# s4's quarter sums on ScalarE's queue, x11 t4 as the fourth quarter product, and first products by pairs of row tiles

## The chip, the cores and the metric

The kernel runs on one core of a Trainium2 chip. The metric is the device time of one launch in microseconds. Three runs before the change took 1567.93, 1563.51 and 1567.34 us, a median of 1567.34 us.

## What is computed

```python
def reference(a, b, alpha):        # a, b: 4096 x 4096 float32, alpha = 0.01
    x = np.matmul(a, b)
    return np.where(x > 0, x, alpha * x)
```

## The kernel before

**Seven products for eight.** Outside its first block the kernel works through 15 regions of the output, each 1024 x 1024 and named (g, j) by its block row and block column, in the order of the list `regions`: (0, 1) (0, 2) (0, 3), then (1, 2) (1, 0) (1, 1) (1, 3), (2, 2) (2, 0) (2, 3) (2, 1), (3, 2) (3, 0) (3, 1) (3, 3). A region is a 2 x 2 block product, A in blocks a11, a12, a21, a22 of 512 rows by 2048 of K, B in blocks B11 to B22 of 2048 by 512. It is done by Winograd's form of Strassen's scheme: sums s1 to s4 of A's blocks, sums of B's blocks made in place on VectorE (`b_sum`, L561), and seven block products instead of eight, numbered 0 to 6 in the code and called first to seventh here where the code does so (`sixth_in_quarters`, `seventh_in_quarters`). All operands are float16, made from the float32 inputs on the way in.

One block product is 64 matmuls (L722) of a 128 x 128 tile of A against 512 columns of B: two tiles `k` of K (`ks`), eight chunks `c` in each, four row tiles `mt`. Each row tile has a PSUM bank of its own. Two sets of four banks alternate: `y` of a region are at `ybank`, `z` at `zbank`, and the next region's `ybank` is this one's `zbank`. Within a block product the order is chunk by chunk, and the four row tiles inside a chunk, so its first four matmuls want four different banks.

**Quarter products.** In the regions of groups g = 1 to 3 that are neither the last of their group nor the last of all, the seventh product (s4 times B22) is done by the same scheme once more, on quarters of 256 rows by 1024 of K and 1024 by 256: seven quarter products of 16 matmuls of 256 columns (`quarter_product`, L673) from quarters x, sums `sx(1)` to `sx(4)` of them, quarters b and sums `t(1)` to `t(4)` of them. In six of these nine regions, (1, 0) (1, 1) (2, 0) (2, 3) (3, 0) (3, 1), the sixth product (a22 times B21) is done in quarters too; the code calls that `both`. The text calls the last region of groups 1 and 2, (1, 3) and (2, 1), turning: there A's next block row is fetched by GpSimd's queue (L130) and transposed on VectorE (L139) between the other steps.

The quarter sums of a22 and s4 are made once a group, in the region that opens it, and kept in DRAM (`kept_qa`, `kept_qs`, stored by L658). The `both` regions load them again (`load_sums`, L667): a22's before product 3, s4's inside `sixth_in_quarters`, by `following(n)`, each of 512 KB into the room of a sum that the sixth has finished with. So a load of s4's sum waits for TensorE: sum 4 for the sixth's second quarter product, sum 2 for the fourth, sum 1 (in the room of `sq[4]`) for the fifth, sum 3 for the sixth.

**The seventh in quarters, before**, is seven quarter products in this order: x01 b10 onto y (banks 0 and 1, left columns); x00 b00 into `one`; sx4 b11 onto y (banks 0 and 1, right columns); sx2 t2 into `one`; sx1 t1 into `other`; sx3 b01 into `one`; x11 t4 onto y (banks 2 and 3, left columns). Between them ScalarE copies `one` out (L798, L801, L806) and VectorE adds `other` (L803, L807), then adds all four banks of y into the result (L810). `one` is bank 3 of `z` in the `both` regions and bank 0 in the three that open a group, `other` is bank 2. These are banks that the next region's first product writes. After it the code fetches B22 for the next region (`fetch_b`, on GpSimd's queue, L505, or SyncE's, L502, for the column whose float16 form is kept) and loads the sum s2 again (`load_s2`, L692).

**Queues.** The order of every engine is the order of the code, written out by hand; nothing is scheduled. Loads from `kept_q`, output stores (L820 in `leave`), and `load_s2` all stand in SyncE's queue (SP), in the code's order, and each waits there for its own data and room. GpSimd's queue (POOL) has the loads from the inputs that change type. ScalarE (ACT) issues two loads at the very start and none after that.

The adds that free `z` after product 1, `add(u1, z)`, and the others of that form are L815; product 3 writes these banks again.

Of the kernel before, what the change touches and what calls it, by code (L numbers as in the profile page):

```python
# [24 lines left out]
KC = 8  # L25
# [21 lines left out]
def kernel(  # L47
# [16 lines left out]
    nc = tc.nc  # L64
# [23 lines left out]
    x = small_pool.tile([P, 8], FP32, name="x")  # L88
# [114 lines left out]
    def new_bank(i):  # L203
        return psum_pool.tile([P, NT], FP32, name="ps", tag=f"ps{i}")
# [126 lines left out]
    order = [("b", 0), ("a", 0, 0, 1), ("a", 1, 0, 1), ("a", 2, 0, 1), ("a", 3, 0, 1)]  # L331
# [3 lines left out]
    for what, i, *more in order:  # L335
        if what == "a":
            r, tiles = more
            k = slice(r * rw, (r + 1) * rw)
# [7 lines left out]
    both = []  # L346
# [98 lines left out]
    for i in range(1, len(steps)):  # L445
        t, h, u, first, last = steps[i]
# [16 lines left out]
        t, h, u, first, last = steps[i]  # L463
# [90 lines left out]
    def operand(g, name, k):  # L554
        if name[0] == "s":
            return s[g, name, k]
        return at[g, int(name[1]) - 1, 2 * (int(name[2]) - 1) + k]
# [61 lines left out]
    kept_q = {name: dram_pool.tile([4, P, QUARTER], DT, name=f"kept_q{name}") for name in ("a22", "s4")}  # L619
# [42 lines left out]
        make(3, (0, 0), (1, 0), SUB)  # L662
        make(4, (0, 1), 2, SUB)

    def load_sums(name, to, which):
        for n in which:
            nc.sync.dma_start(to[n], kept_q[name][n - 1])  # L667

    def quarter_product(xq, yq, to, first=False):
        for c in range(KC):  # L670
            for m in range(2):
                rows = slice(m * P, (m + 1) * P)
                nc.tensor.matmul(  # L673
                    to[m], xq[:, c // 2, rows, c % 2], yq[:, c, :],
                    start=first and (c, m) == (0, 0), stop=c == KC - 1, skip_group_check=True,
                )

    def into(bank):
        return [bank[:, m * HALF:(m + 1) * HALF] for m in range(2)]
# [24 lines left out]
    for i, (g, j) in enumerate(regions):  # L704

        ks = (1, 0) if in_quarters else (0, 1)
        late_s2 = in_quarters
# [4 lines left out]
        zbank = 4 - ybank  # L712

        def product(n, banks, first):
            name, half, nt = PRODUCTS[n]
            todo = [(k, c) for k in ks for c in range(KC)]
            order = [(mt, k, c) for k, c in todo for mt in range(MT)]
            if final and n == 6:
                order = [(mt, k, c) for mt in range(MT) for k, c in todo]
            for mt, k, c in order:  # L720
                t = operand(g, name, k)
                nc.tensor.matmul(  # L722
                    banks[mt], a_cols(t, c, mt, t is first_a), B(half, nt, k)[:, c, :],
                    start=first and (k, c) == todo[0], stop=(k, c) == todo[-1], skip_group_check=not first,
                )
# [12 lines left out]
        def sixth_in_quarters(pairs, banks, v, y, tq, sq):  # L738


            b = quarters_of_b(i, 1, 0)
            x = quarters_of_a(g, "a22")
            one, other, third, fourth = banks
            t = lambda n: b_quarter(tq[n])
            sx = lambda n: a_quarter(sq[n])
            next_t, next_s = {}, {}
            y7 = quarters_of_b(i, 1, 1)

            def more(r, n, t):
                block = pairs[r][:, :, n * HALF:(n + 1) * HALF]  # L750
                nc.vector.tensor_add(block, pair(t), block)

            def following(n, room=None):
                next_s[n] = new_a16() if room is None else room
                load_sums("s4", next_s, (n,))

            quarter_product(x[0, 0], b[0, 0], into(one), True)
            add(v[:2], y[:2])
            more(0, 0, one)
            add(v[2:], y[2:])  # L760
            quarter_product(sx(1), t(1), into(other), True)
            more(1, 1, other)
            following(4)
            next_t[2] = tq[1]
            quarter_product(x[0, 1], b[1, 0], into(fourth), True)
            leave(v, 1, 1)
            quarter_product(sx(2), t(2), into(one))
            following(2)
            more(0, 1, one)
            sums_of_b(y7, next_t, (2,))  # L770
            more(0, 0, fourth)
            quarter_product(sx(4), b[1, 1], into(other))
            following(1, sq[4])
            next_t[4] = tq[2]
            sums_of_b(y7, next_t, (4,))
            more(0, 1, other)
            quarter_product(sx(3), b[0, 1], into(one))
            following(3)
            more(1, 0, one)
            more(1, 1, one)  # L780
            quarter_product(x[1, 1], t(4), into(third), True)
            more(1, 0, third)
            next_t[1] = tq[4]
            sums_of_b(y7, next_t, (1,))
            return next_t, next_s

        def seventh_in_quarters(y, one, other, tq, sq):

            pairs, kept = new_c(side)
            b = quarters_of_b(i, 1, 1)  # L790
            x = quarters_of_a(g, "s4")
            t = lambda n: b_quarter(tq[n])
            sx = lambda n: a_quarter(sq[n])
            block = lambda r, n: pairs[r][:, :, n * HALF:(n + 1) * HALF]
            onto = lambda r, n: [y[2 * r + m][:, n * HALF:(n + 1) * HALF] for m in range(2)]
            quarter_product(x[0, 1], b[1, 0], onto(0, 0))
            quarter_product(x[0, 0], b[0, 0], into(one), True)
            nc.scalar.copy(block(0, 0), pair(one))  # L798
            quarter_product(sx(4), b[1, 1], onto(0, 1))
            quarter_product(sx(2), t(2), into(one))  # L800
            nc.scalar.copy(block(0, 1), pair(one))  # L801
            quarter_product(sx(1), t(1), into(other), True)
            nc.vector.tensor_add(block(0, 1), pair(other), block(0, 1))  # L803
            quarter_product(sx(3), b[0, 1], into(one))
            for n in (1, 0):
                nc.scalar.copy(block(1, n), pair(one))  # L806
            nc.vector.tensor_add(block(1, 1), pair(other), block(1, 1))  # L807
            quarter_product(x[1, 1], t(4), onto(1, 0))
            for mt in range(MT):
                nc.vector.tensor_add(kept[mt], y[mt], kept[mt])  # L810
            return kept

        def add(acc, banks):
            for to, bank in zip(acc, banks):
                nc.vector.tensor_add(to, bank, to)  # L815
# [25 lines left out]
        y = [new_bank(ybank + mt) for mt in range(MT)]  # L841
        z = [new_bank(zbank + mt) for mt in range(MT)]
# [5 lines left out]
        both = in_quarters and not first_of_group  # L848
# [34 lines left out]
        u2_pairs, u2 = keep(y, 1 - side)  # L883
# [8 lines left out]
        if in_quarters:  # L892
            t = x_pool.tile([P, 4, QUARTER], DT, name="q", tag="x")
            tq, sq = {2: t[:, 0], 1: t[:, 1], 4: t[:, 2]}, {4: t[:, 3]}
# [7 lines left out]
        z = [new_bank(zbank + mt) for mt in range(MT)]  # L902
# [20 lines left out]
        if turning:  # L923
            new_s(g + 1, "s1")
            t = new_s(g + 1, "s2").rearrange("p k c m e -> p (k c m e)").bitcast(BF16)
            a21 = measure(i + 1, 0, 1, 0, t.rearrange("p (n w) -> p n w", n=4))
            a21.begin()
        if both:
            tq, sq = sixth_in_quarters(u2_pairs, [new_bank(zbank + mt) for mt in range(MT)], v, y, tq, sq)
# [12 lines left out]

        if not both:
            product(5, z, False)
            add(u2, z)
        fetch_b(i + 1, [(1, 0)], (1, 0) if both else ks)
        fetch_a(1, 1, slice(3))
        leave(u2, 1, 0)
# [8 lines left out]

        if in_quarters:

            kept_c = seventh_in_quarters(y, new_bank(zbank + (3 if both else 0)), new_bank(zbank + 2), tq, sq)  # L960
            fetch_b(i + 1, [(1, 1)], (1, 0))
            new_s(g, "s2")
            load_s2(g, 1)
            leave(kept_c, 0, 1)
        else:
            product(6, y, False)
            fetch_b(i + 1, [(1, 1)], ks)
            if final:
                even = nc.values_load(good[0:1, 0:1], min_val=0, max_val=1)
            _, kept_c = new_c(side)  # L970

            def store(mt):
                nc.sync.dma_start(place(g, 0, mt, j, 1), kept_c[mt])

            for mt in range(MT):
                nc.scalar.copy(kept_c[mt], y[mt])  # L976
                leaky(kept_c[mt])
                if not (final and mt == MT - 1):
                    store(mt)
# [5 lines left out]
    with inputs.Else():  # L985
        for m in range(M // RM):
            a_blocks = []
            for u in range(KU):
                t = a_pool.tile([P, KC // 2, RM, 2], BF16, name="a", tag=f"a{u // 2 + 1}{m % 2 + 1}")
                for mt in range(0, MT, 2):  # L990
                    to = lambda t0, t1: [t[:, :, (mt + t0) * P:(mt + t1) * P, :]]
# [4 lines left out]
            for n in range(N // NT):  # L996
                banks = [new_bank(n % 2 * 4 + mt) for mt in range(MT)]
                cols = slice(n * NT, (n + 1) * NT)
                for u in range(KU):
                    t = b_pool.tile([P, KC, NT], BF16, name="b", tag=f"b{u // 2 + 1}{n % 2 + 1}")  # L1000
# [8 lines left out]
                for mt in range(MT):  # L1009
                    t = c_pool.tile([P, 2, NT], FP32, name="c", tag=f"c{side}")[:, 0]  # L1010
# [38 lines left out]
```

## Time and the profile before

| | |
|---|---|
| median of three runs | 1567.34 us (1563.51 to 1567.93) |
| the profiled execution | 1564.15 us, span 1562.3 us |
| granted TensorE clock, mean | 0.999 |
| TensorE matmuls, busy | 1547.7 us, 7995 matmuls |
| VectorE busy | 1126.4 us |
| ScalarE busy | 373.5 us |
| 512-column matmuls, L722, from A and from sums | 752.6 + 503.2 us, 3456 + 2304 matmuls |
| loads of s4's quarter sums | 24 of 512 KB, median 10.4 us from issue to landing |
| loads of a22's quarter sums | 24 of 512 KB, median 6.3 us |

Times in the profile count from the span's start. A line of the timeline has start, length, engine, source line, operation and tiles, and in brackets the idle time before it with what ended it; a matmul's length is that of its whole pass through the array, so neighbours overlap, and the pace is read from the starts. In the windows view a line has, for each stretch, the busy time of each engine, then the granted clock, the DMA share and GB/s.

### The profile page before, as it was taken

How to read it: one execution, taken by the hardware profiler on the slowest of the kernel's cores; microseconds unless marked ns; L12 is line 12 of the kernel's file. 1: busy time of each engine (PE TensorE's matmuls, PEld its weight loads, DVE VectorE, ACT ScalarE, POOL GpSimd, SP SyncE). 2: the span in 40 equal slices, each digit the busy share in tenths (PEclk: the TensorE clock that was granted, in tenths of full speed). 3: DMA queues.
4: the chain of work that ended last, by engine and by line, in shares of the span. 5: the costliest groups of instructions: out<-in, count | busy, mean ns of one | idle time of the engine just before them, and what ended most of it. 6: DMA issues, size and time to landing. Idle time of an engine off the chain costs nothing. (4 is left out here: it accounts for less than half of the span.)

```text
span 1562.3 us, 20105 instructions
## 1 busy us (share of the span) xinstructions
PE 1547.7 (99%) x7995; PEld 779.9 (50%) x7995; DVE 1126.4 (72%) x1265; ACT 373.5 (24%) x390; POOL 299.7 (19%) x482
## 2 busy tenths in 40 slices
PE   9999999999999999999999999999999999999998
PEld 4444444444445456474444546547444454745543
DVE  4368758777984676965799587685879959678474
ACT  2201243612100314301111241420022143151230
POOL 5641110244002011023401102012340110202100
PEclk9999999999999999999999999999999999999999
DMA  9999694999829789499985959969996794978902
GB/s 243 187 212 193 140 285 149 186 202 189 294 63 272 171 180 273 125 256 213 185 291 144 273 126 231 228 150 275 208 220 225 176 266 105 272 179 187 272 27 84
DMA packets 206056, 310.75 MB, mean 199 GB/s; under 512 B 18049, under 2 KB 155521, under 8 KB 199042
## 3 DMA queue, kind: packets, MB, share of 16 engines
q0 software_dynamic: 149376, 141.59, 56.9%
q1 hardware_dynamic: 56290, 167.41, 28.9%
q8 instruction: 64, 1.05, 0.3%
q10 hardware_dynamic: 288, 0.39, 0.1%
q14 instruction: 38, 0.31, 0.1%
HBM read 354.42 MB, written 94.37 MB: 287 GB/s over the span
## 5 line engine op out<-in xcount | busy, mean ns | idle before, releaser
L722 PE MATMUL ps<-b,a 128*128 128x512 f16 x3456 | 752.6, 379 | 0.2 <-DVE c L815 0.2
L722 PEld LDWEIGHTS <-a 128*128 128x128 f16 x3456 | 338.2, 98 | 406.4 <-issue 0.8
L722 PE MATMUL ps<-b,s 128*128 128x512 f16 x2304 | 503.2, 379 | 0.0
L722 PEld LDWEIGHTS <-s 128*128 128x128 f16 x2304 | 225.4, 98 | 271.9
L561 DVE TENSOR_TENSOR b<-b 128x4096 f16<-128x4096 f16 x112 | 252.8, 2291 | 111.3 <-DMA b<-in_b_dram 104.5
L505 POOL DMA_DIRECT2D b<-in_b_dram x184 | 136.4, 746 | 931.4 <-PE ps L722 625.4
L735 ACT COPY c<-ps 128x512 f32<-128x512 f32 x180 | 92.3, 598 | 459.5 <-PE ps L722 398.3
L139 DVE STREAM_TRANSPOSE a<-a 128x512 uint32<-128x512 uint32 (+2 forms) x120 | 126.9, 1104 | 85.0 <-DMA a<-in_a_dram 83.9
L130 POOL DMA_DIRECT2D a<-in_a_dram x252 | 137.4, 552 | 201.4 <-DVE a L139 119.3
L815 DVE TENSOR_TENSOR c<-ps,c 128x512 f32<-128x512 f32 x156 | 97.1, 683 | 87.2 <-PE ps L722 58.1
L307 DVE SCALAR_TENSOR_TENSOR c<-c 128x512 f32<-128x512 f32 x240 | 149.6, 688 | 12.7 <-ACT c L976 10.0
L227 ACT ACTIVATE sq<-b 128x2048 bf16<-128x2048 f16 x64 | 119.2, 1909 | 113.5 <-DVE sq L236 89.3
L279 PE MATMUL ps<-b,a 128*128 128x512 f16 x512 | 113.0, 379 | 2.4 <-DVE part L318 1.3
L227 ACT ACTIVATE sq<-a 128x2048 bf16<-128x2048 f16 x48 | 89.0, 1910 | 109.2 <-DVE sq L236 87.5
L673 PEld LDWEIGHTS <-q 128*128 128x128 f16 x960 | 92.7, 98 | 16.5 <-DMA q<-kept_qs 5.8
L279 PEld LDWEIGHTS <-a 128*128 128x128 f16 x512 | 49.7, 98 | 63.5 <-issue 3.8
L798 ACT COPY c<-ps 128x512 f32<-128x512 f32 x9 | 5.3, 587 | 257.9 <-PE ps L673 257.9
L673 PE MATMUL ps<-b,q 128*128 128x256 f16 x480 | 56.4, 273 | 0.6 <-DMA q<-kept_qs 0.4
L673 PE MATMUL ps<-q,q 128*128 128x256 f16 x384 | 45.4, 273 | 0.8 <-DMA q<-kept_qs 0.8
L239 DVE TENSOR_TENSOR sq<-sq 128x2048 bf16<-128x2048 bf16 x27 | 33.1, 1226 | 17.1 <-ACT sq L227 17.1
L673 PEld LDWEIGHTS <-s 128*128 128x128 f16 x432 | 42.3, 98 | 5.5
L803 DVE TENSOR_TENSOR c<-ps,c 128x512 f32<-128x512 f32 x9 | 6.2, 692 | 43.7 <-issue 43.7
(94 smaller groups left out, 715.2 us busy)
## 6 DMA issues: line engine op xcount, KB each, us to landing
b<-in_b_dram POOLq DMA_DIRECT2D x192, 512.0 KB, 14.6
out_dram<-c SPq DMA_DIRECT2D x240, 256.0 KB, 6.0
a<-in_a_dram POOLq DMA_DIRECT2D x244, 128.0 KB, 5.3
b<-kept SPq DMA_DIRECT2D x24, 1024.0 KB, 7.9
s<-kept_s SPq DMA_DIRECT2D x18, 1024.0 KB, 7.3
q<-kept_qa SPq DMA_DIRECT2D x24, 512.0 KB, 6.3
q<-kept_qs SPq DMA_DIRECT2D x24, 512.0 KB, 10.4
b<-in_b_dram POOLq DMA_DIRECT2D x24, 256.0 KB, 9.4
```

Source lines behind the costliest of these rows:

```text
L130: nc.gpsimd.dma_start(a16[32 * q:32 * q + 32], src.rearrange("(g i) w -> i g w", i=32))
L139: nc.vector.transpose(part.rearrange("p c m e -> p c (m e)").bitcast(U32) .rearrange("p c (g i) -> p g c i", i=32), src[:, :, i * n:(i + 1 ...
L227: nc.scalar.activation(to, self.parts[n], SQUARE)
L239: nc.vector.tensor_add(total, total, self.held[3])
L279: nc.tensor.matmul(ps, a_cols(at[0, h, u], c, mt, (h, u) == (0, 0)), bt[0, u, nt][:, c, :], start=first, stop=last,)
L307: nc.vector.scalar_tensor_tensor(t, t, alpha, t, op0=MULT, op1=MAX if alpha <= 1 else MIN)
L505: nc.gpsimd.dma_start(t[:, c:c + 4, :], b_rows(j, u, c, 4, nt, g > 0))
L561: nc.vector.tensor_tensor(f(to), f(x0), f(x1), op)
L673: nc.tensor.matmul(to[m], xq[:, c // 2, rows, c % 2], yq[:, c, :], start=first and (c, m) == (0, 0), stop=c == KC - 1, skip_group_check=True,)
L722: nc.tensor.matmul(banks[mt], a_cols(t, c, mt, t is first_a), B(half, nt, k)[:, c, :], start=first and (k, c) == todo[0], stop=(k, c) == t ...
L735: nc.scalar.copy(kept[mt], banks[mt])
L815: nc.vector.tensor_add(to, bank, to)
```

## The change

Five edits go together.

1. `load_sums` takes a queue, and the loads of s4's quarter sums inside the sixth are issued by ScalarE.
2. In a region that follows one with quarter products, the first product (n == 0) goes, for each `k`, over all chunks for row tiles 0 and 1, then over all chunks for row tiles 2 and 3. The matmuls are the same.
3. In the seventh, x11 t4 moves from seventh to fourth place, so sx2 t2, sx1 t1 and sx3 b01 come one place later and sx3 b01 is last.
4. After a sixth that is not in quarters the adds of `z` go from bank 3 down to bank 0.
5. `one` is bank 3 of `z` in all nine regions.

```diff
-    def load_sums(name, to, which):
+    def load_sums(name, to, which, queue=nc.sync):
         for n in which:
-            nc.sync.dma_start(to[n], kept_q[name][n - 1])
+            queue.dma_start(to[n], kept_q[name][n - 1])
...
             order = [(mt, k, c) for k, c in todo for mt in range(MT)]
+            if n == 0 and late_s2:
+                order = [(mt, k, c) for k in ks for mts in ((0, 1), (2, 3)) for c in range(KC) for mt in mts]
...
-                load_sums("s4", next_s, (n,))
+                load_sums("s4", next_s, (n,), nc.scalar)
...
             quarter_product(sx(4), b[1, 1], onto(0, 1))
+            quarter_product(x[1, 1], t(4), onto(1, 0))
             quarter_product(sx(2), t(2), into(one))
...
             nc.vector.tensor_add(block(1, 1), pair(other), block(1, 1))
-            quarter_product(x[1, 1], t(4), onto(1, 0))
             for mt in range(MT):
...
             product(5, z, False)
-            add(u2, z)
+            add(u2[::-1], z[::-1])
...
-            kept_c = seventh_in_quarters(y, new_bank(zbank + (3 if both else 0)), new_bank(zbank + 2), tq, sq)
+            kept_c = seventh_in_quarters(y, new_bank(zbank + 3), new_bank(zbank + 2), tq, sq)
```

`late_s2` is true in a region whose predecessor ended in quarter products.

## The prediction

> **What bounds the kernel now.** I read the page first: TensorE is busy nearly all the time, so only its idle time can be won. The chain that ended last is two pieces at the very end and says nothing. The waits of TensorE come next; of its rows this one belongs to quarter products that load s4's sums.
>
> ```profile
> PE 1547.7 (99%) x7995; PEld 779.9 (50%) x7995; DVE 1126.4 (72%) x1265; ACT 373.5 (24%) x390; POOL 299.7 (19%) x482
> ...
> PE ps L673 <- DMA q<-kept_qs: 1.7, 5, 0.5
> ...
> DMA to landing us min/median/max: 7.4/10.6/12.8
> ```
>
> The wait is counted as the gap between modelled matmul ends and so is too small; the third line (the view of the tile kept_qs) says how long these loads take. The timeline of TensorE shows the true size, by start times. This is the seventh product of region (1, 1), from its second product on:
>
> ```profile
> 684.74 3.66 PE L673 MATMUL ps<-b,s 128*128 128x256 f16 x32
> 688.23 1.91 PE L673 MATMUL ps<-b,q 128*128 128x256 f16 x16
> 690.64 1.92 PE L673 MATMUL ps<-q,q 128*128 128x256 f16 x16 [0.50 <-DMA q<-kept_qs]
> 692.93 1.92 PE L673 MATMUL ps<-q 128*128 128x256 f16 x16 [0.38 <-DMA q<-kept_qs]
> 694.72 1.92 PE L673 MATMUL ps<-b,q 128*128 128x256 f16 x16
> 696.48 1.91 PE L673 MATMUL ps<-q,s 128*128 128x256 f16 x16
> 698.22 27.79 PE L722 MATMUL ps<-b,a 128*128 128x512 f16 x128
> ```
>
> A quarter product takes (688.23 - 684.74) / 2 = 1.745 us when nothing is late. Five lie between 688.23 and 698.22: 9.99 us instead of 8.73, so 1.26 us are lost, before sums 2, 1 and 3. The same stretch in the six regions with both products in quarters: 593.67 to 603.44, 688.23 to 698.22, 975.38 to 984.63, 1069.42 to 1078.75, 1355.33 to 1364.66, 1449.44 to 1458.55. Less 8.73 each, these lose 1.04, 1.26, 0.52, 0.60, 0.60 and 0.38, **4.40 us** in all. The three regions that open a group lose nothing here. Who issues these loads, and when:
>
> ```profile
> 676.20 0.32 SPq L667 DMA_DIRECT2D q<-kept_qs  x1
> 677.57 2.14 SPq L820 DMA_DIRECT2D out_dram<-c  x4
> 679.80 3.71 SPq L667 DMA_DIRECT2D q<-kept_qs  x3
> 687.41 2.14 SPq L820 DMA_DIRECT2D out_dram<-c  x4
> ```
>
> Sum 2 leaves at 679.80, 0.3 us after the fourth quarter product of the sixth (677.75 to 679.50) has given its tile free, and is behind four output stores in one queue; it releases TensorE at 690.64, 10.8 us later. In region (2, 3) the stores also hold up the issue itself, by about 1 us.
>
> **x11 t4 goes ahead of the three late users.** No matmul is added: 16 of them change place. Sums 2, 1 and 3 are released after the sixth's products 4, 5 and 6 and needed at places 4, 5 and 6 of the seventh; these become 5, 6 and 7, so each has 7 x 1.745 = 12.2 us instead of 10.5. Worst case (1, 1), with landings read from the starts above: sum 2 needed at 679.50 + 12.2 = 691.7, there at 690.64; sum 1 at 681.25 + 12.2 = 693.5, there at 692.93; sum 3 at 682.99 + 12.2 = 695.2, there at 694.72. Margins 1.1, 0.6, 0.5 us, even if the queue changes nothing. All 4.40 us go. Sum 4 keeps its 12.2 us and was not late. The moved product needs t4, which VectorE makes at 682.04 (L645), and now starts near 690: covered by 7 us; bare it would cost the 1.22 us of that row. The bank `one` is now copied out two products before it is reused the first time, not one: cheaper, worth nothing since no wait stood there.
>
> **The loads move to ScalarE's queue.** 24 issues of 0.32 us. ScalarE has nothing between the copies of v and the seventh's first copy (in the waits it idles up to 29.7 us for it), and the last load leaves near 683.2, 5 us before that copy at 688.4: nothing. Behind a waiting load stands only that copy; without cover it would hold TensorE by the excess, once a region. On SP the stores of v and u2 no longer stand between or behind loads; nobody waits for them but the reuse of v's tile, at the same copy. The trace has no such load on ScalarE's queue while stores run, so latency is bounded: not better than 7.4 us, the least of the kept_qs row, and not worse than 12.8, its greatest. 12.8 would leave 0.6 us of stall for a load, the slack being 12.2; I take 9 to 11, since the stores ahead go away and 2 MB of loads and 1 MB of stores still have to pass.
>
> The Trainium skill, DMA: Bandwidth & Descriptors, section Issuing engines are not separate DMA queues, speaks against this edit: transfers of all issuers run on the same 16 engines and only issue time is saved. By it this edit alone is worth about the 1 us of late issue in (2, 3) and the like in (3, 1). The trace leans the other way, as sum 2 lands behind four stores of its own queue; no run here has the second queue. The sum above does not need it.
>
> **Pairs of row tiles, and the bank.** Now the last product before the next region fills `one`. Its two copies (L806, 1.07 us) end some 1.3 us later, the add that frees `other` (L807, 0.69 us, behind the first copy) about 1.7 us later. In the old order of rows the next product would need banks 2 and 3 after 0.43 and 0.65 us: 1.1 us lost, nine times. By pairs it needs them after 16 x 0.216 = 3.45 us. Nothing is lost. Needing all of a B tile's first pass 3.4 us sooner is free, as that tile's fetch is issued 32 us ahead (POOL's timeline: 666.30, for the product at 698.22). Alternating two banks rather than four is bounded by the quarter products, which alternate halves of one bank at 0.109 us per 256 columns: no cost.
>
> **Knock-on.** b[0, 1] is now read last, so POOL's fetch of B22's k = 0 tile, issued at 696.94, waits for the last product: in (1, 1) that ends at 698.22 - 1.26 = 696.96, so 0.5 us later by the clock. VectorE's four adds and four leaky passes at the region's end slip by 2 to 3 us into an idle stretch of 5 us or more. The reversed adds are the same four instructions. All nothing, as long as these queues stay as full or as idle as now.
>
> **What is late next.** Ending 1.26 us sooner in (1, 1) puts TensorE closer to the turning region (1, 3), whose product 3 waits already:
>
> ```profile
> 739.66 1.00 PE L722 MATMUL ps<-b,a 128*128 128x512 f16 x3
> 740.88 13.33 PE L722 MATMUL ps<-b,a 128*128 128x512 f16 x61 [0.22 <-DVE c L815]
> ...
> 732.15 2.11 DVE L139 STREAM_TRANSPOSE a<-a 128x512 uint32<-128x512 uint32 x2 [0.50 <-DMA a<-in_a_dram]
> 736.37 2.09 DVE L139 STREAM_TRANSPOSE a<-a 128x512 uint32<-128x512 uint32 x2 [2.10 <-DMA a<-in_a_dram]
> 738.39 2.44 DVE L815 TENSOR_TENSOR c<-ps,c 128x512 f32<-128x512 f32 x4
> ```
>
> The adds that free the banks stand behind transposes that wait for A, and A stands in POOL's queue behind B:
>
> ```profile
> 670.00:680.00 10.00, 10.00 (x82) 7.81 (x81) 6.48 (x11) 0.00 (x0) 1.48 (x2) 1.00 1.19 192
> 710.00:720.00 10.00, 10.00 (x48) 4.51 (x46) 3.52 (x3) 2.05 (x4) 1.98 (x4) 1.00 1.23 213
> ```
>
> The last but one column, the DMA share, is above 1 from 660 to 730: the transfers do not come sooner because TensorE does. So (1, 3) waits 1.26 us more, and that gain is given back. The same place in (2, 1): adds 1117.32 to 1119.76, the fourth bank needed at 1120.84, 1.08 us to spare against a gain of 0.60: kept. The other regions reach these adds 4 to 7 us early.
>
> **Sum.** 4.40 - 1.26 = 3.1 us. Against the profiled execution: 1564.15 (span 1562.3 and 1.85 around it) becomes 1561.0. The median shown is 3.2 us above that execution, so I forecast 1567.34 - 3.1 = **1564.2**.
>
> **Rivals.** (a) All 4.4 us stay won, because A also comes sooner in (1, 3), the queue of B being shorter by what ScalarE's row takes over: 1562.9. Against it: the bytes are the same. 0.17. (b) The three times before differ by 4.4 us, and the profiled one is among the short. If the long ones have loads some 0.7 us later (six regions x 0.7 = 4.2 us), the median run loses 8.6 us here and gives back 2: 1560.7. For it: the stall is the excess of a latency over a fixed slack, so it grows one for one; against: no trace of a long run. 0.18. (c) The gain does not arrive: the loads come as much later as their place, or every region returns it as (1, 3) does: 1567.3. 0.08. (d) Slower: three queues share the engines, and the kept_qs loads take longer than the 12.2 us that they now have. Each excess is paid once a region; at 14.5 us, six times 2.3 = 13.8 us stand in place of 4.4: 1576.7. It decides from 12.95 us on (12.2 and the mean loss of 0.73 now). Against it: the greatest in the trace is 12.8, with stores ahead. 0.07.
>
> **How the numbers follow.** My forecast has the remaining 0.50. A measurement can tell about 0.3%, 4.7 us, from no change. Faster by more: (b), half of (a), whose gain lies at this bound, and 0.04 of the forecast's spread, 0.30. Slower: (d), 0.07. The rest, 0.63, within. The range goes from the lowest time shown less the whole gain, 1563.5 - 4.4 = 1559.1, to (c) with the highest time shown, 1567.9; it leaves out (d) and little else.
>
> **What would show it.** In the profile after, the kept_qs wait is gone from TensorE's waits and the seven quarter products stand 1.745 us apart; the loads are issued on ACT; the wait for L815's successor in (1, 3) grows from 0.22 towards 1.5 us. Wrong: quarter products still waiting for kept_qs, a wait of the first product of a region on the copy or add of banks 2 and 3, or (1, 3) unchanged.

## The result, and the profile after

| | before | after |
|---|---|---|
| median of six runs each | 1564.17 us (1563.40 to 1567.93) | 1558.91 us (1557.83 to 1560.85) |
| the profiled execution | 1564.15 us, span 1562.3 us | 1560.85 us, span 1559.1 us |
| TensorE matmuls, busy | 1547.7 us | 1546.7 us |

The ratio is 0.9962, with an interval of 0.9948 to 0.9975: faster by 5.3 us. The forecast was 1564.2 us, and the time is 0.2 us below the range, which began at 1559.1. Later comparisons put before at 1565.0 to 1565.1 us (18, 17 and 9 runs) and after, once more, at 1558.68 us (six runs, ratio 0.9959, 0.9946 to 0.9971).

In the profile after, the wait for kept_qs is gone from TensorE's waits. The row for the adds has grown in its place, and the loads stand on ScalarE's queue (q10 in the page). Two lines of the page, of its queues and of its DMA issues, the last with the median us from issue to landing:

```profile
q10 hardware_dynamic: 3744, 12.98, 2.2%
...
q<-kept_qs ACTq DMA_DIRECT2D x24, 512.0 KB, 8.2
```

TensorE's waits, in us in total, times, and the longest:

```profile
PE ps L725 <- DVE c L818: 1.0, 4, 0.4
```

In the median the loads land in 8.2 us, where the same row of the page before has 10.4. Followed by their semaphores one by one, they took 6.9 to 9.6 us, one 11.2, all under the slack of 12.2 (in each profile three of the 24 have no landing on record). The view of the tile kept_qs, which the prediction reads for these loads, is not of the loads alone: it counts the 12 stores that write kept_qs (L658) with the 24 loads. The 12.8 us that the prediction takes as the greatest load of before is such a store; the loads there took 7.4 to 11.5.

The same place as in the prediction, the seventh of region (1, 1), in TensorE's timeline. L725 and L818 are the L722 and L815 of before.

```profile
686.50 1.91 PE L673 MATMUL ps<-b,q 128*128 128x256 f16 x16
688.25 1.91 PE L673 MATMUL ps<-q,s 128*128 128x256 f16 x16
...
693.49 1.91 PE L673 MATMUL ps<-b,q 128*128 128x256 f16 x16
695.24 27.79 PE L725 MATMUL ps<-b,a 128*128 128x512 f16 x128
```

ScalarE's timeline has the four loads in one row, issued one after another as the sixth frees their room:

```profile
674.48 7.31 ACTq L667 DMA_DIRECT2D q<-kept_qs  x4
```

From 686.50 to 695.24 the five quarter products take 8.74 us, where before they took 9.99: nothing waits, and x11 t4 (q,s) is the second of them. The next product starts at 695.24 with banks 0 and 1 and runs 128 matmuls without a stop, so the pairs of row tiles cover the late copies. All six regions look like this; what is left of these waits is 0.01 us.

The turning regions came out otherwise than forecast. In (1, 3) product 3 now waits for nothing, where 0.57 us were lost before and 1.26 us more were expected. TensorE's timeline there, then VectorE's:

```profile
736.68 13.98 PE L725 MATMUL ps<-b,a 128*128 128x512 f16 x64
```

```profile
731.47 2.11 DVE L139 STREAM_TRANSPOSE a<-a 128x512 uint32<-128x512 uint32 x2 [0.90 <-DMA a<-in_a_dram]
733.50 2.44 DVE L818 TENSOR_TENSOR c<-ps,c 128x512 f32<-128x512 f32 x4
```

The adds start at 733.50, 4.9 us sooner than the 738.39 of before, while TensorE is only 3.0 us ahead (736.68 against 739.66). So in this pair of executions the transfers of A did come sooner. They vary, though: three profiles of before have the first of these adds at 736.06 to 739.90, two of after at 733.50 and 736.02. In (2, 1), which was said to have 1.08 us to spare, TensorE loses instead, 1.68 us over the region. The two timelines again:

```profile
1116.05 0.38 PE L725 MATMUL ps<-b,a 128*128 128x512 f16 x1 [0.38 <-DVE c L818]
```

```profile
1113.33 2.11 DVE L139 STREAM_TRANSPOSE a<-a 128x512 uint32<-128x512 uint32 x2 [2.16 <-DMA a<-in_a_dram]
1115.35 2.44 DVE L818 TENSOR_TENSOR c<-ps,c 128x512 f32<-128x512 f32 x4
```

It is the same wait in another place: the adds stand behind transposes that wait 2.16 us for A.

### The profile page after: what moved, and what is told of

Its sections match the earlier page's. It is cut to its first block, busy times and chain, and to the rows that moved or that the text cites. A ratio compares the mean times of both kernels' runs of the same rounds, so it can differ in the third digit from the quotient of the medians.

```text
span 1559.1 us, 20114 instructions
## 1 busy us (share of the span) xinstructions
PE 1546.7 (99%) x7995; PEld 781.4 (50%) x7995; DVE 1126.9 (72%) x1265; ACT 373.6 (24%) x390; POOL 300.4 (19%) x482
## 5 line engine op out<-in xcount | busy, mean ns | idle before, releaser
L725 PE MATMUL ps<-b,a 128*128 128x512 f16 x3456 | 752.8, 379 | 1.0 <-DVE c L818 1.0
L725 PEld LDWEIGHTS <-a 128*128 128x128 f16 x3456 | 338.2, 98 | 407.5 <-issue 2.2
L725 PE MATMUL ps<-b,s 128*128 128x512 f16 x2304 | 503.2, 379 | 0.0
L725 PEld LDWEIGHTS <-s 128*128 128x128 f16 x2304 | 225.4, 98 | 271.9
L818 DVE TENSOR_TENSOR c<-ps,c 128x512 f32<-128x512 f32 x156 | 97.1, 681 | 88.7 <-PE ps L725 58.4
L807 DVE TENSOR_TENSOR c<-ps,c 128x512 f32<-128x512 f32 x9 | 6.2, 691 | 54.3 <-issue 54.3
## 6 DMA issues: line engine op xcount, KB each, us to landing
b<-in_b_dram POOLq DMA_DIRECT2D x192, 512.0 KB, 15.1
```

Of the source, the lines that this page charges most:

```text
L725: nc.tensor.matmul(banks[mt], a_cols(t, c, mt, t is first_a), B(half, nt, k)[:, c, :], start=first and (k, c) == todo[0], stop=(k, c) == t ...
```

## The experiments

Two sums are used for each profile, both read from the starts of TensorE's matmuls. q is what the sevenths in quarters lose to late loads of s4's sums. T is what the products 3 and 4 of (1, 3) and (2, 1) lose to adds behind the transposes.

**The queue alone**, `only_queue`: before, with edit 1.

```diff
-                load_sums("s4", next_s, (n,))
+                load_sums("s4", next_s, (n,), nc.scalar)
```

> The kernel before with the loads of s4's quarter sums on ScalarE's queue and nothing else changed. Theory Q (the queue is what counts: in the profile after, these loads take 6.9 to 9.6 us instead of 10.7 to 11.5, less than the 10.5 us that the old order gives them): all 4.4 us of quarter-product waits vanish, ratio about 0.997. Theory P (the place is what counts, a second queue only interleaves on the same 16 engines): the loads land as late as before, 10.7 to 11.5 us, the 4.4 us stay, ratio 1.000.

Measured: 1558.39 us (1557.75 to 1561.41), ratio 0.9960 (0.9947 to 0.9972). The row of the loads in the page:

```profile
q<-kept_qs ACTq DMA_DIRECT2D x24, 512.0 KB, 8.2
```

The queue alone brings as much as the whole change. The median load lands 2.2 us sooner than the 10.4 of before, and no wait for kept_qs is left at a slack of 10.5 us.

Which loads gain tells why. Sum 4's load is issued ahead of the four stores of v, the other three behind them. Here is region (2, 3), first sum 4's load and then the other three, in before and then in `only_queue` (DMA view, last number the median us to landing):

```profile
q<-kept_qs SPq DMA_DIRECT2D x1, 512.0 KB, 7.5
q<-kept_qs SPq DMA_DIRECT2D x3, 512.0 KB, 10.4
```

```profile
q<-kept_qs ACTq DMA_DIRECT2D x1, 512.0 KB, 7.0
q<-kept_qs ACTq DMA_DIRECT2D x3, 512.0 KB, 7.8
```

Over the six regions sum 4's load takes 7.7 us in the mean in both kernels. Those of sums 2, 1 and 3 go from 9.6, 10.7 and 11.0 to 7.6, 8.4 and 9.3. So only the loads that stood behind stores in SP's queue land sooner. The stores pay for it: the last of v's four lands 7.7 to 9.2 us after its issue in before and 11.4 to 15.1 here.

q is 0.44, all of it in (1, 1), and there TensorE waits for a copy of ScalarE (L798), not for a load. ScalarE's timeline has this copy waiting for an output store:

```profile
687.42 0.58 ACT L798 COPY c<-ps 128x512 f32<-128x512 f32 x1 [29.47 <-DMA out_dram<-c]
```

The second store of v landed at 687.32, 11.5 us after its issue, and the copy writes the tile that v leaves. This is the reuse of v's tile that the prediction named without a price. In after the copy has one quarter product more before TensorE wants its bank, and no wait shows.

**The place without the queue**, `no_queue`: after, without edit 1, so edits 2 to 5 together.

```diff
-                load_sums("s4", next_s, (n,), nc.scalar)
+                load_sums("s4", next_s, (n,))
```

> The kernel after with these loads back on SyncE's queue; the place of x11 t4, the bank, the order of row tiles and of the adds as after. Theory P: latency stays at 10.7 to 11.7 us as before, the slack is 12.2, so no quarter product waits, and the time is that of after, ratio about 0.996. Theory Q: some waits stay, above all in (1, 1) where the margin is 0.5 us; ratio 0.997 to 1.000.

Measured: 1560.12 us (1558.80 to 1561.98), ratio 0.9966 (0.9954 to 0.9978). The loads are as late as before and a wait for them is left (the row of the page, then TensorE's waits):

```profile
q<-kept_qs SPq DMA_DIRECT2D x24, 512.0 KB, 10.3
```

```profile
PE ps L673 <- DMA q<-kept_qs: 0.5, 1, 0.5
```

q is 1.42 us, in (2, 3) and (3, 0), 0.7 us in each. The 12.2 us of slack hold most loads, not all (those of sums 1 and 3 took 12.3 to 12.7 us in these two regions): the margins of 0.5 to 1.1 us that were read in one region of one execution are too thin for the others.

**The old order of rows**, `old_order`: after, without edit 2.

```diff
-            if n == 0 and late_s2:
+            if False:
```

> The kernel after with the first product's old order, four row tiles inside a chunk. By the working of the prediction its third and fourth matmul want banks 2 and 3 at 0.43 and 0.65 us while the add and the copies free them 1.7 and 1.3 us after the last quarter product: a wait of 1.1 to 1.3 us in each of nine regions, 10 us in all, ratio to before about 1.003. If the wait is hidden by something, the time is that of after.

Measured: 1568.84 us (eleven runs, 1567.93 to 1572.76), ratio 1.0025 (1.0016 to 1.0034), 10.2 us over after of the same comparison. TensorE's waits, then its timeline and then VectorE's at the end of a seventh (L811 is the add of `other`, L807 before):

```profile
PE ps L725 <- DVE c L811: 8.7, 9, 1.0
```

```profile
507.98 0.59 PE L725 MATMUL ps<-b,a 128*128 128x512 f16 x2
509.55 5.79 PE L725 MATMUL ps<-b,a 128*128 128x512 f16 x26 [0.97 <-DVE c L811]
```

```profile
508.80 0.69 DVE L811 TENSOR_TENSOR c<-ps,c 128x512 f32<-128x512 f32 x1 [1.62 <-ACT c L810]
```

Two matmuls run on banks 0 and 1; the third wants bank 2, which the add frees at 509.49 (508.80 + 0.69). From start to start that is 509.55 - 507.98 = 1.57 us, where two matmuls take 0.43: 1.14 us lost, in each of nine regions, 10.3 us. Edit 2 is thus what makes edit 3 pay: the place without the pairs is slower than before, even with the loads on ScalarE's queue. This profile also has 2.5 us of T in (1, 3).

**After once more**, `after_again`: no edit.

> The changed kernel unaltered, for a second profile and its time beside the others on one chip. Theory A (the wait of product 3 in the turning regions is a race between A's transfers and TensorE that falls out differently from run to run): the waits at the adds in (1, 3) and (2, 1) differ from the first profile's 0 and 1.7 us, the sum of the two between 0 and 3 us. Theory B (it is set by the change): 0 in (1, 3) and 1.7 in (2, 1) again. Quarter products stand 1.745 us apart in both.

Measured: 1558.68 us (1557.27 to 1559.49). q is 0. T is 1.12 us, all in (1, 3), with nothing in (2, 1): the reverse of the first profile of the same kernel.

**Before once more, twice**, `before_again` and `before_third`: no edit, one profiled execution each.

> The kernel before unaltered, for a second profile. Theory L (the waits for kept_qs are an excess of transfer time over a fixed slack and so vary from run to run, from about 4 us up): its waits in the seventh differ from the first profile's 4.1 us, between 4 and 9 us in all. Theory S (they are the same in every execution, and the spread of the times of before has another source): 4.1 us again within 0.5.

> The same once more, a third profile of the kernel before. Theory L: again another sum between 4 and 9 us. Theory S: 4.1 us.

Measured: 1565.72 and 1564.00 us. Their rows of TensorE's waits for the loads:

```profile
PE ps L673 <- DMA q<-kept_qs: 1.6, 3, 1.2
```

```profile
PE ps L673 <- DMA q<-kept_qs: 2.4, 4, 1.9
```

By the starts q is 4.52 and 5.46 us, and T 2.09 and 0.15. The same kernel thus loses other amounts in other regions each time it runs.

**The loads left out**, `before_no_loads` and `after_no_loads`: the quarter sums of s4 are not loaded in the `both` regions; the tiles of a22's sums are read in their place.

```diff
-                next_s[n] = new_a16() if room is None else room
-                load_sums("s4", next_s, (n,))
+                next_s[n] = sq[n]
```

> The kernel before with the 24 loads of s4's quarter sums left out: the seventh product in quarters uses a22's sums, which stand in the same rooms, so six regions hold other numbers. No quarter product can wait for kept_qs. Theory L (in unprofiled runs these waits are larger than the 4.1 us that the profiled execution shows, and they are all that the change removes): it comes out where the kernel after stands, 1558 to 1559, 6 us under before. Theory E (the waits are 4.1 us in every run, and some 2 us of the gain come from another edit, the pairs or the bank): about 1561, with the rest of the way to 1558.7 missing.

> The kernel after with the same 24 loads left out in the same way. Theory L: the kernel after has none of these waits left, so leaving the loads out wins nothing at the seventh; with 12.6 MB less on the DMA engines the waits of the turning regions may shrink by 1 us: 1557.5 to 1558.7. Theory E: 2 us under before_no_loads.

Measured: 1558.59 us (1557.61 to 1559.54), ratio 0.9952 (0.9936 to 0.9967), and 1558.62 us (1557.61 to 1559.31), ratio 0.9951 (0.9935 to 0.9966). q and T are 0 in both profiles. So before loses 1565.03 - 1558.59 = 6.4 us to having these loads. That this is their lateness and not their 12 MB of traffic follows from after, which still makes them and stands at 1558.68. After is 0.1 us above its own bound: of these waits nothing that can be measured is left to win. And since the two kernels without the loads are equal, the other four edits win nothing where no load can be late; what they win in `no_queue` is the time that they give the loads.

**The adds ahead of A's fetch.** `fetch_a(0, 0)` holds the transposes that the adds stand behind. `adds_first` and `before_adds_first` move it behind them in every region, `adds_first_late` only in groups 1 to 3.

```diff
-        fetch_a(0, 0)
         product(1, z, True)
         add(u1, z)
+        fetch_a(0, 0)
```

> The kernel after with the fetch and transposes of A's next block row moved behind the adds that free product 3's banks, so that these adds no longer stand behind transposes that wait for transfers. Theory A (what is left in the turning regions is a race of A's transfers against TensorE, 0 to 3 us a run): the waits on the adds vanish in (1, 3) and (2, 1), those of product 2 on B's sums may stay; 1557.5 or less, about 1 us under after, with a smaller spread. Theory B (the waits are set by the order of VectorE elsewhere and come back as waits on the later transposes, product 4 or the next region): no change.

> The same move in the kernel before. If the turning regions cost before about what they cost after, it gains as much here as in adds_first, some 1 us (ratio 0.9994); if they cost nothing before, because TensorE comes late there anyway, it gains nothing. A gain of 3 us or more would say that the spread of the times before comes from here and not from the loads of s4's sums.

> The kernel after with A's fetch and transposes behind the adds in groups 1 and 2 only; in group 0, where the move cost 11 us in (0, 3), the order is that of after. Expected: no wait at the adds in (1, 3) and (2, 1), and so the time of after less the mean of what these waits cost in unprofiled runs. The profiles of after have 1.1 and 1.7 us there, but after and after_no_loads tie at 1558.6 and the latter's profile has none, so the mean is small: 1557.8 to 1558.7, ratio to before 0.995 to 0.996.

Measured: `adds_first` 1568.25 us (1565.77 to 1570.45), ratio 1.0012 (1.0002 to 1.0022); `before_adds_first` 1575.13 us (1571.47 to 1578.58), ratio 1.0056 (1.0036 to 1.0076); `adds_first_late` 1559.10 us (1558.34 to 1560.24), ratio 0.9962 (0.9949 to 0.9976). In the first, T is 0 as meant, but (0, 3) loses 11.0 us, where the transposes now hold up a sum of B. TensorE's timeline, and then the windows view (last columns: clock, DMA share, GB/s):

```profile
380.68 16.86 PE L725 MATMUL ps<-b,s 128*128 128x512 f16 x64 [7.97 <-DVE b L561]
397.38 13.98 PE L725 MATMUL ps<-b,a 128*128 128x512 f16 x64
```

```profile
372.00:380.60 8.60, 0.70 (x4) 0.10 (x1) 4.22 (x4) 2.05 (x4) 3.78 (x7) 0.75 1.08 224
380.70:385.70 5.00, 5.00 (x12) 1.77 (x13) 5.00 (x4) 0.00 (x0) 1.14 (x3) 0.50 1.07 172
```

The wait is 8.1 us by the starts; the other 2.9 us come after it, for the product behind it takes 397.38 - 380.68 = 16.70 us instead of 13.81, at half the clock at first. `adds_first_late` avoids this and has neither q nor T (span 1557.7), yet it is not faster than after: T costs nothing that the unprofiled runs show. `after_no_loads` says the same: its profile has these adds 5 us early in both regions, and its time is that of after. `before_adds_first` has q of 7.98 us in its profile, the largest seen, and no T, but (0, 3) loses 8.0 us there. So it does not answer what the turning regions cost before.

**Sum 2 asked for later**, `late_sum2`: before, with the loads of sums 2 and 3 exchanged, so that sum 2 leaves after the sixth's sixth product and has 7.0 us of slack.

```diff
-            following(2)
+            following(3)
...
-            following(3)
+            following(2)
```

> The kernel before with the calls following(2) and following(3) exchanged, so that sum 2 takes the room that is free after the sixth's sixth quarter product and sum 3 the one free after the fourth. Sum 2 then has four quarter products, 7.0 us, until it is needed, instead of six, 10.5 us. If the wait is latency less slack, one for one, sum 2 waits 3.5 us more than its latency of 10.7 to 11.5 already made it, 3.7 to 4.5 us in each of six regions, and sums 1 and 3 are there by then: 22 to 27 us in place of the 4 to 8 us of before, time 1580 to 1587. If the loads go faster when asked for later, less than 10 us.

Measured: 1597.20 us (two runs, 1595.19 and 1599.21), ratio 1.0206 (1.0185 to 1.0227): 32 us slower. TensorE's waits, its timeline in region (1, 0), and the windows view of the same stretch:

```profile
PE ps L673 <- DMA q<-kept_qs: 25.8, 6, 5.8
```

```profile
593.77 1.91 PE L673 MATMUL ps<-b,q 128*128 128x256 f16 x16
599.61 3.59 PE L673 MATMUL ps<-q,q 128*128 128x256 f16 x16 [3.93 <-DMA q<-kept_qs]
603.00 2.96 PE L673 MATMUL ps<-q 128*128 128x256 f16 x16
```

```profile
595.00:599.00 4.00, 0.68 (x7) 0.36 (x4) 0.00 (x0) 0.00 (x0) 1.48 (x2) 0.91 1.13 293
599.00:604.00 5.00, 4.39 (x21) 3.15 (x22) 0.00 (x0) 0.59 (x1) 0.00 (x0) 0.50 1.17 262
```

The six waits are 4.0 to 6.0 us, 26.8 us in all: each region pays what its load exceeds the slack by, within 0.3 us (sum 2's loads took 10.7 to 12.7 us), as the prediction had it. But the time lost in these sevenths is 39.95 us. The two quarter products behind the wait take 3.39 and 2.80 us (599.61 to 603.00, and on to 605.80) instead of 1.745, at a granted clock of 0.50. That makes up the other 13 us.

**The account.** Each span less q and T:

| kernel | span | q | T | rest |
|---|---|---|---|---|
| before | 1562.3 | 4.40 | 0.57 | 1557.3 |
| before_again | 1563.9 | 4.52 | 2.09 | 1557.3 |
| before_third | 1562.2 | 5.46 | 0.15 | 1556.6 |
| before_no_loads | 1556.7 | 0 | 0 | 1556.7 |
| after | 1559.1 | 0.01 | 1.68 | 1557.4 |
| after_again | 1557.7 | 0 | 1.12 | 1556.6 |
| only_queue | 1559.5 | 0.44 | 3.15 | 1555.9 |
| no_queue | 1560.2 | 1.42 | 1.28 | 1557.5 |
| after_no_loads | 1557.0 | 0 | 0 | 1557.0 |
| adds_first_late | 1557.7 | 0 | 0 | 1557.7 |

The rest is 1555.9 to 1557.7 us, so these two waits account for nearly all that sets the profiled executions apart. The other four profiles fit once their own losses are taken off as well: 1556.5 for `old_order` (10.3 at the banks, 2.5 of T, and 1.7 to a lower clock behind it), 1557.6 for `adds_first`, 1557.6 for `before_adds_first` and 1557.4 for `late_sum2`. T seems to be smaller in runs without a profile: the profiled executions of after, after_again, only_queue and no_queue, all with T, are the longest of their lists, and adds_first_late, without T, gains nothing on after.

## Why the prediction was wrong, point by point

**What was right.** The waits named are where the gain comes from, and all of them went. The pairs cover what they were said to cover: 1.14 us nine times was measured against 1.1. None of the knock-ons shows a wait: the adds in reverse, the bank `one`, the later fetch of B22, ScalarE's issues in after. The queue was left out of the sum as unneeded, and its latency was taken as 9 to 11 us; the median of the loads is 8.2 in after and 8.2 alone, a little better than that. One knock-on does show where the queue moves alone: the reuse of v's tile, 0.44 us in one region.

**The base, 2.3 us.** The sum was taken from the median of three, 1567.34; that of 17 runs is 1565.03. The three differ by 4.4 us, and two of them lie in the upper part of what before shows (1562.46 to 1570.88). The other two terms are errors of the gain itself, which was forecast at 3.1 us and measured at 5.3, and at 6.3 in the later comparison.

**The first term, 2.0 us.** "All 4.40 us go" took the loss from one profiled execution. Four profiles with the loads on SP's queue at their old place have 4.40, 4.52, 5.46 and 7.98, and the unprofiled runs lose 6.4 in the median. Rival (b), at 0.18, was this mechanism, with 8.6 lost and 2 given back. That its net gain of 6.6 is close to the 6.4 measured is luck: 8.6 was too much, and nothing was seen to be given back. "Even if the queue changes nothing" failed as well: 1.42 us stay in the profile without the queue.

**The second term, 1.26 us.** "The transfers do not come sooner because TensorE does", and so (1, 3) "waits 1.26 us more", failed. The adds in (1, 3) came 4.9 us sooner in the first profile. T is 0.57, 2.09 and 0.15 us in three profiles of before and 1.68 and 1.12 in two of after, once in the one region and once in the other. It is a race between A's transfers and TensorE that comes out otherwise in each execution, not a debt that is repaid one for one. From these few profiles a small debt can't be excluded: T is 0.9 us in the mean before and 1.4 after. Its price in unprofiled runs is nothing that could be measured. That also fells the 1.08 us to spare in (2, 1), read from one execution.

Put right, the sum is 1565.03 - 6.4 - 0 = 1558.6. The three errors add to 5.6 us of the 5.3 by which the forecast was too high; the rest is what medians of different comparisons differ by.

**The claim that the place suffices** holds only in part: without the queue 1.42 us of waits stay in the profile, and the time is 1.4 us above after. The claim that the queue alone is worth little, which the prediction took from the rule below and doubted itself, fell outright. The Trainium skill, DMA: Bandwidth & Descriptors, section Issuing engines are not separate DMA queues, has only issue time saved by a second issuer, at most about 1 us here (q is 0.60 and 0.38 in (2, 3) and (3, 1), the regions with a late issue); the measurement decides for 6.6 us (1565.01 - 1558.39) and for loads that land 2.2 us sooner. What changed is what stands ahead of them: sum 2 was behind four output stores in SP's queue and is behind none in ScalarE's. That the stores are the cause, and not something else about the second queue, is borne out by sum 4's load, which stands ahead of the stores and takes 7.7 us in either queue. No run took the stores away.

**The rivals.** (d), slower above 12.95 us, did not occur, since the loads got faster. `late_sum2` shows that its mechanism exists and that its price would be too low for long waits: one of 4 to 6 us cost 1.7 to 2.8 us more in clock. (c) did not occur either. (a) had the right sign on A's transfers and too small a gain.

## What to carry to other kernels

A wait for a transfer that is near its slack is a distribution: read it from several executions, or leave the transfer out to bound it, before a size goes into a sum. Look at what stands ahead of a late load in its own queue: here the loads behind 1 MB of stores landed about 2 us sooner on a queue without them, and the stores landed later. When an operand's place is moved ahead, look at once at which bank the next product needs first; here that would have cost 10 us, twice what the change won.

## What was not expected of the hardware

The median kept_qs load landed in 8.2 us on ScalarE's queue (`only_queue`) and in 10.4 on SP's (before), with the same bytes moved. The load issued ahead of v's stores took 7.7 us in the mean on either.

A gap of TensorE of 3.8 us or more was followed by 3.4 to 5.9 us at a granted clock of 0.50: after each of the six waits of `late_sum2` (gaps of 3.82 to 5.83 us; the quarter product behind each has a pass of 2.87 to 3.60 us instead of 1.91, and in the mean 2.2 us more are lost for each), after the 7.97 us in `adds_first` (2.9 us more) and the 6.22 us in `before_adds_first` (1.7 us more). The gaps up to 1.86 us in the profiles of before were not: the quarter products behind them keep 1.745 us. Nor were one of 1.84 and three of 0.22 us in a row in `only_queue`. But in `old_order` one of 1.19 and three of 0.22 us, in (1, 3), were followed by 3.4 us at 0.50, which cost 1.7 us. The Trainium skill, TensorE: Matmul & The Clock Gate, Part 1, gives half the clock after an idle window of about 3.4 us. The gaps of 3.8 us and more agree with it; the four in `old_order` do not, as matmuls start between them. No profile has a gap between 1.9 and 3.8 us.

The size of a wait in the waits view is that between modelled ends of matmuls. For many small waits it is far too small: 1.7 us of before's 4.4, 1.6 of 4.52 and 2.4 of 5.46. For six long ones it is nearly whole: 25.8 of 26.8.
